# Low parts of w_in, key sums and both halves of a head's first keys made on VectorE instead of POOL

## The chip, the cores and the metric

The kernel runs on one core of a Trainium2 chip. Its metric is the device time of one execution in microseconds (us). Before the change it is 2476.84 us, the median of three runs (2475.95 to 2477.19). One further execution was taken by the hardware profiler; the profile's numbers come from that one.

The engines, by the names of the profile: PE is TensorE (matrix products; PEld are its weight loads), DVE is VectorE, ACT is ScalarE, POOL is GpSimd, SP is SyncE, which issues nearly all DMAs here. In the code they are `T`, `V`, `S`, `G` and `nc.sync`. Each engine runs its own queue of instructions strictly in order.

## The reference, cut to what matters

One layer of a diffusion backbone on 2048 latent tokens of width 1024, with 256 context tokens ahead:

```
h = modulate(rmsnorm(x), shift, scale)
p = h @ w_in                          # 1024 x 3584: gates fwd, gates bwd, v, q, out gate (512 each), u, v of the gMLP
k_f, k_b = sigmoid(-gate_f), sigmoid(-gate_b);  f = sigmoid(gate)
o = scan_fwd(q, k_f, v, f_f) + scan_bwd(q, k_b, v, f_b)      # gated linear recurrence, 4 heads of 128 x 128 state
o_hg = rmsnorm(o) * silu(p_gate);  o_mlp = spatial gating of u, v
x = x + g1 * (concat(o_hg, o_mlp) @ w_out)
x = x + g2 * conv_ffn(modulate(rmsnorm(x)))                  # up-projection, 3x3 depthwise conv, down-projection
return rmsnorm(x) * norm_final
```

All in fp32.

## The kernel before

**Split products.** TensorE's fast fp32 format (F32R) keeps fewer bits. So each factor is split in a high part, a rounded copy made by ScalarE, and a low part, what the copy lost: `lo = raw - hi` (`split`, line 129). A product is then three products: hi·hi, hi·lo, lo·hi (`mm3`, and the same three lines in `run_banks`, line 534).

**Stages.** By the trace's times: modulation vectors and context tokens (0 to some 180 us); projections and heads (to 1010 us); output projection and second norm (to some 1260 us); up-projection with the convolution (to 2048 us); down-projection and final norm (to the end). The change lies in the first two.

**Projections.** w_in is taken 128 columns at a time, a *key* in the code. `split_w` loads such a column (raw, 128 partitions x 8 x 128), lets ScalarE make `whi` and another engine `wlo`. There are two buffers for the pair: `w_free` holds the free ones. `run_banks` goes through a list of *banks*, products of one column with 512 (context: 256) tokens, 24 products each, with the result in a PSUM bank `pj`. At each bank it makes sure that this column and the one after it are split, so the split of a column waits until the products of the column two before it are done. A head's two gate columns are interleaved (`[ff[0], fb[0], ff[1], fb[1]]`, line 1018), so both buffers are held until the third of these four banks is done, and the column after them has one bank's time.

**Who makes the low part.** `split_w` counts its calls in `w_n` and takes VectorE for the first seven and every odd one below 20, POOL for the others (line 223). Two early calls name VectorE themselves.

**A head.** `hg` (line 775) is a generator whose steps are put between the banks' products by a pump, after waits in TensorE time that are written in the code (`yield 6.5`). First `kd`, the sum of both directions' keys, and `Q`, queries times gates of each direction; then score products with `kd` for the diagonal; then seven levels `B = 1, 2, 4 ... 64`. Each level has score products of `K` and `Q` (copied into `sc` through a mask by `V.copy_predicated`), an update of `Q` in place, new keys `K2` from `level_keys`, and the next totals. `level_keys` (line 562) makes the keys for B up to 32 in two halves, a = 0 and 1. Of each half one part is multiplied by totals, a = 0 on VectorE and a = 1 on POOL, and the other part is copied by ScalarE. At B = 1 the totals are the gates `F` themselves, and the copies are pinned in ScalarE's program order.

**Beside it** a second pump runs background work between the products: x's second half, modulation rows (`ada_block`, line 918), w_out and w_down times their gates (`w_out_ops`, line 950, which loads a gate row `g` from DRAM; `w_down_ops`, line 966).

**What sets the order.** When the program is built, a planner goes through it with times of its own and puts each instruction in its engine's queue when its inputs are ready by those times, earlier code first among ready ones. `pin` ties an instruction behind all earlier code of its engine. On the chip the queues are fixed: an instruction that must wait holds all behind it on its engine.

Of the kernel before, what the change touches and what calls it, by code (L numbers as in the profile page):

```python
# [24 lines left out]
CTX = 256  # L25
HW = 512
# [57 lines left out]
def tile_trunk(ctx, tc, x, c, cx, c_ctx, w_ada, b_ada, norm_mix, norm_ffn, w_in, hg_norm, sgu_g, sgu_b,  # L84
               w_sp, b_sp, w_out, w_up, conv_w, conv_b, w_down, norm_final, masks, out):
    nc = tc.nc
    V, S, G, T = nc.vector, nc.scalar, nc.gpsimd, Tensor(nc.tensor)
# [41 lines left out]
    def split(hi, lo, raw, eng=None, keep=lambda i: i):  # L129

        keep(S.copy(hi, raw))  # L131
        (eng or G).tensor_sub(lo, raw, hi.bitcast(F32))  # L132
# [56 lines left out]
    with es1:  # L189
# [13 lines left out]
        def bank(tag):  # L203
            return ps.tile([P, 512], F32, tag=tag, name=tag, bufs={"pj": 3, "sc": 2, "mi": 3}[tag])
# [1 line left out]
        def raw_tile():  # L206
            return p1.tile([P, D], F32, tag="raw", name="raw", bufs=3)

        w_n, w_raw, w_free = [0], {}, [0, 1]

        def load_raw(key):
            raw = raw_tile().rearrange("p (k c) -> p k c", c=P)
            ld(raw, w_in[:, key[0]:key[0] + P].rearrange("(k p) c -> p k c", p=P))
            w_raw[key] = raw

        def split_w(key, eng=None):
            if key not in w_raw:
                load_raw(key)
            raw, at = w_raw.pop(key), w_free.pop(0)
            hi = p1.tile([P, NK, P], F32R, tag=f"whi{at}", name="whi", align_bytes=AL)  # L220
            lo = p1.tile([P, NK, P], F32R, tag=f"wlo{at}", name="wlo", align_bytes=AL)
            w_n[0] += 1
            split(hi, lo, raw, eng or (V if w_n[0] < 8 or w_n[0] < 20 and w_n[0] % 2 else G))
            return hi, lo, at

        def x_sums():
            return pm.tile([P, 8], F32, tag="xss", name="xss", bufs=2)

        def x_square(xs, ss, i0=0, keep=pin):
            for i, xt in enumerate(xs):  # L230
                jk = pm.tile([P, D], BF16, tag="acc", name="xjk")
                keep(S.activation(jk, xt, AF.Square, accum_out=ss[:, i0 + i:i0 + i + 1]))

        def x_scale(xs, ss, keep=pin):

            r = rstd(pm, ss[:, :len(xs)], len(xs), 1.0 / D, keep=keep)
            for i, xt in enumerate(xs):
                keep(V.tensor_scalar(out=xt, in0=xt, scalar1=r[:, i:i + 1], scalar2=None, op0=ALU.mult))
# [18 lines left out]
        wts, rows, pa, nxt = {}, {}, {}, {}  # L257
# [5 lines left out]
        def load_ada(g, qs=(0, 1)):  # L263

            for q in (qs,) if isinstance(qs, int) else qs:
                t = wa[g // 2][:, 4 * (g % 2) + 2 * q:4 * (g % 2) + 2 * q + 2, :]
                wts[g, q] = t.rearrange("p a (b e) -> p (a b) e", e=512)
                ld(wts[g, q], wv[:, 4 * q:4 * q + 4, g * 512:(g + 1) * 512])
# [3 lines left out]
        def ada_products(g, k0, k1):  # L272
            if k0 == 0:
                pa[g] = bank("pj")
            for k in range(k0, k1):
                T.matmul(pa[g][:2, :], cs2[:, k, :], wts[g, k // 4][:, k % 4, :], start=(k == 0), stop=(k == 7))

        def ada_rows(g, tag):
            rows[g] = pm.tile([2, 512], F32, tag=tag, name="rows", bufs=2)
            S.copy(rows[g], pa.pop(g)[:2, :])  # L280

        def ada_columns(g):
            o = 128 + 16 * g
            for j in range(4):
                T.transpose(small[:, o + 2 * j:o + 2 * j + 2], rows[g][:, j * P:(j + 1) * P], ident[:2, :2])
            put_ada(g, small[:, o:o + 8].rearrange("p (j w) -> p w j", w=2), 0, 2)
# [36 lines left out]
        def ctx_products(c, ks):  # L323
            hi, lo, _ = nxt[c, CTX]
            pj = opened[c, CTX]
            for k in ks:
                mm3(pj[:, :CTX], hi[:, k, :], lo[:, k, :], chl[:, k, :], cll[:, k, :], k == 0, False)
# [4 lines left out]
        with tc.manual_schedule():  # L332
            load_ada(2)
            for i in range(2):
                ld(xc[i], cx[0][i * P:(i + 1) * P, :])
            vr = pm.tile([66, P], F32, tag="gu", name="vr", bufs=2)
            for a, n, r0 in ((norm_mix[0], 8, 0), (b_ada[0, 0:2 * D], 16, 50), (norm_ffn[0], 8, 8), (hg_norm[0], 4, 16),
                             (sgu_g[0], 4, 20), (sgu_b[0], 4, 24), (conv_b[0], 22, 28)):
                S.dma_start(vr[r0:r0 + n, :], a.rearrange("(r p) -> r p", p=P))
            load_ada(0)  # L340
            load_raw((0, CTX))
            load_ada(1)
            load_ada(3)
            load_raw((HW, CTX))
            S.activation(sg, cc, AF.Sigmoid)
            V.tensor_mul(cs2.rearrange("p k w -> p w k"), cc, sg)
            ss = x_sums()
            x_square(xc, ss, keep=lambda i: i)
            ada_products(2, 0, 4)
            small = bank("sc")  # L350
            T.transpose(small[:, :66], vr, ident[:66, :66])
            V.tensor_copy(vec, small[:, :50])
            V.tensor_copy(bc[:, :8], small[:, 50:58])
            V.tensor_scalar(out=bc[:, 8:], in0=small[:, 58:66], scalar1=1.0, scalar2=None, op0=ALU.add)
            ada_products(2, 4, 8)
            ada_rows(2, "ot")
            x_scale(xc, ss, keep=lambda i: i)
            ada_products(0, 0, 4)
            ada_columns(2)
            nxt[0, CTX] = split_w((0, CTX), V)  # L360
            for k in range(NK):
                for i in range(2):
                    o = (k % 2) * 256 + i * P
                    T.transpose(pct[k // 2][:, o:o + P], xc[i][:, k * P:(k + 1) * P], ident)
            ada_products(0, 4, 8)
            ada_rows(0, "ot")
            ada_sums(1, 0, 5)
            load_raw((2 * HW, CTX))
            for i in range(4):
                ld(xg[i], x_rows[i])  # L370
            ada_products(3, 0, 1)
            ada_columns(0)
            ada_products(3, 1, 8)
            ctx_mod(0)
            ada_sums(1, 5, 8)
            for k in range(1, 4):
                ctx_mod(k)
                ada_sums(0, k - 1, k)
            nxt[HW, CTX] = split_w((HW, CTX), V)
            ss0 = x_sums()  # L380
            x_square(xg[:1], ss0, keep=lambda i: i)
            ada_rows(3, "ot")
            ada_ones(1, small, 256)
            ada_columns(3)
            opened[0, CTX] = bank("pj")
            ctx_products(0, range(4))
            for k in range(4, NK):
                ctx_mod(k)
            ada_sums(0, 3, 8)
            ada_ones(0, small, 288)  # L390
# [171 lines left out]
        def level_keys(K, B, tot):  # L562

            W, nb = TH, TH // B
            K2 = pk.tile([P, 2, W], F32, tag="K", name="K2", bufs=2, align_bytes=AL)
            if B == P // 2:
                n = W // (2 * B)
                src = [[2 * B, n], [B, 2], [1, B]]
                t = view(tot, nb + 1, [[2, n], [-(nb + 1), 2], [0, B]])
                V.tensor_mul(view(K2, 0, [[2 * B, n], [W + B, 2], [1, B]]), view(K, 0, src), t)  # L570
                S.copy(view(K2, W, [[2 * B, n], [B - W, 2], [1, B]]), view(K, W, src))
                return K2
            n = W // (4 * B)
            for a in range(2):
                src = [[4 * B, n], [B, 2], [1, B]]
                t = view(tot, nb + 1 + 2 * a, [[4, n], [-(nb + 1), 2], [0, B]])
                e = G if a else V
                keep = pin if B == 1 else lambda i: i
                e.tensor_mul(view(K2, a * (2 * B + W), [[4 * B, n], [W + B - 2 * a * W, 2], [1, B]]),
                             view(K, a * 2 * B, src), t)  # L580
                keep(S.copy(view(K2, a * 2 * B + (1 - a) * W, [[4 * B, n], [B - W + 2 * a * W, 2], [1, B]]),
                            view(K, W + a * 2 * B, src)))
            return K2
# [60 lines left out]
        for h in range(NH):  # L644
            F, K, vt = sets[h % 2]
# [128 lines left out]

        def hg(hh, h, F, K, qs, vt, sgt):
            kd = ph.tile([P, TH], F32, tag="T1", name="kd")
            G.tensor_add(kd, K[:, 0, :], K[:, 1, :])
            Q = ph.tile([P, 2, TH], F32, tag="Q", name="Q", align_bytes=AL)
            for d in range(2):
                V.tensor_mul(Q[:, d, :], qs, F[:, d, :])  # L780
# [11 lines left out]
            for l, B in enumerate(LV):  # L792
# [13 lines left out]
                K = level_keys(K, B, tot)  # L806
# [522 lines left out]
    B = [[xah[:, i] if i < NR else None, xal[:, i] if i < NR - 1 else None] for i in range(7)]  # L1329
# [186 lines left out]
    for n, (u, i) in enumerate(prods):  # L1516
# [7 lines left out]
        hi, lo = u.A[i]  # L1524
# [37 lines left out]
    V = Kept(nc.vector, pin)  # L1562
# [243 lines left out]
```

## Time and profile before

| | us |
|---|---|
| median of three runs | 2476.84 |
| profiled execution | 2477.96 |
| its span, first to last instruction | 2476.2 |
| PE busy | 2421.4 (98%) |
| DVE busy | 1784.7 (72%) |
| ACT busy | 968.2 (39%) |
| POOL busy | 1053.7 (43%) |
| POOL's low parts of w_in, 55 | 135.5 |
| POOL's key sums, 8 | 26.0 |
| POOL's halves of the first keys, 8 | 21.1 |

A row of a group gives line, engine, operation, out<-in by the program's names, shape, count, then busy us, mean ns of one, and after the second bar the idle time of the engine just before these instructions with what ended it. A row of the timeline gives start, duration and, in brackets, the idle time before it and its releaser. Line 132 is the subtraction in `split`, line 131 its copy, line 65 any product. Products are pipelined and their ends modelled, so a product's duration is longer than the distance to the next.

### The profile page before, as it was taken

The page shows a single profiled execution, that of the slowest core. Times are in us where ns is not written, and L with a number is a line of the kernel's source. Part 1 is how long each engine was busy: PE and PEld are TensorE (multiplying, and loading weights), DVE is VectorE, ACT ScalarE, POOL GpSimd, SP SyncE. Part 2 cuts the span into 40 slices and gives each one's busy share as a digit, 9 for nine tenths or more (in the row PEclk, how much of TensorE's full clock was granted, in tenths as well). Part 3 has the DMA queues.
Part 4 walks back from the last instruction along what each step waited for, and adds up shares of the span by engine and source line. Part 5 has one row for each costly group of instructions (what it writes and reads, how often), then busy time and mean ns, then how long its engine had stood idle before and what let it go on. Part 6 is the DMA issues. An engine that isn't in the chain of part 4 may idle for free.

```text
span 2476.2 us, 32805 instructions
## 1 busy us (share of the span) xinstructions
PE 2421.4 (98%) x11859; PEld 2009.7 (81%) x11859; DVE 1784.7 (72%) x2374; ACT 968.2 (39%) x1614; POOL 1053.7 (43%) x866
## 2 busy tenths in 40 slices
PE   7899999999999999999999999999999999999998
PEld 4787888788888888788878888888878888888887
DVE  5766875645765866465699778759999993776876
ACT  3454334434344443244443333334333342432343
POOL 1344232332333433100588787887878770000002
PEclk9999999999999999999999999999999999999999
DMA  8365445573353422768932222472222239834645
GB/s 304 96 191 184 128 137 189 177 261 120 103 182 129 144 99 86 241 210 258 310 106 90 89 80 90 143 273 86 83 93 85 91 101 354 309 120 153 225 149 195
DMA packets 307854, 400.12 MB, mean 162 GB/s; under 512 B 33113, under 2 KB 216161, under 8 KB 304621
## 3 DMA queue, kind: packets, MB, share of 16 engines
q1 hardware_dynamic: 304404, 397.28, 48.3%
q8 instruction: 94, 1.54, 0.3%
q10 hardware_dynamic: 3289, 0.76, 0.1%
q14 instruction: 67, 0.55, 0.1%
HBM read 288.85 MB, written 109.13 MB: 161 GB/s over the span
## 4 chain that ended last, share of the span: by engine, by line
PE 37%; DVE 7%; issue 3%; POOL 2%; ACT 1%; DMA 1%; SPq 0%; POOLq 0%; ACTq 0%; DVEq 0%
PE up L65 23%; PE dn L65 14%; DVE dn L1373 3%; DVE edges L1378 1%; DVE gp L1454 1%; ACT dn L1370 1%; POOL Al L132 0%; DMA yd<-fl 0%; POOL ra L1665 0%; POOL rr L1666 0%; DVE keep L1448 0%; POOL raw L1191 0%; DVE keep L1464 0%; ACT Ah L131 0%; ACT cv L1392 0%
## 5 line engine op out<-in xcount | busy, mean ns | idle before, releaser
L1373 DVE SCALAR_TENSOR_TENSOR dn<-gp,taps,dn 128x1024 f32<-128x1024 f32 x352 | 448.6, 1281 | 21.1 <-ACT dn L1370 17.9
L65 PE MATMUL up<-yf,Ah 128*128 128x512 f32 x1232 | 393.5, 389 | 0.0
L65 PE MATMUL dn<-thl,mhl 128*128 128x512 f32 x1680 | 381.5, 389 | 1.2 <-ACT thl L131 1.2
L132 POOL TENSOR_TENSOR Al<-raw,Ah 128x512 fp32r<-128x512 f32 x264 | 343.0, 1308 | 89.5 <-ACT Ah L131 81.4
L65 PEld LDWEIGHTS dn<-thl,mhl 128*128 128x128 f32 x1680 | 315.0, 188 | 67.7 <-ACT thl L131 2.0
L65 PE MATMUL pj<-xh,whi 128*128 128x512 f32 x896 | 363.8, 406 | 0.0
L65 PE MATMUL pj<-xh,wlo 128*128 128x512 f32 x896 | 350.8, 392 | 1.2 <-DVE wlo L132 1.2
L65 PE MATMUL pj<-xl,whi 128*128 128x512 f32 x896 | 350.3, 391 | 1.2 <-POOL xl L132 1.0
L65 PE MATMUL up<-xah,Al 128*128 128x512 f32 x704 | 275.5, 391 | 3.4 <-POOL Al L132 3.1
L65 PE MATMUL up<-xah,Ah 128*128 128x512 f32 x704 | 274.6, 390 | 0.6 <-ACT Ah L131 0.6
L65 PEld LDWEIGHTS up<-yf,Ah 128*128 128x128 f32 x1232 | 231.2, 188 | 47.9
L131 ACT CAST Ah<-raw 128x512 fp32r<-128x512 f32 x264 | 160.6, 618 | 276.3 <-PE up L65 213.7
L132 POOL TENSOR_TENSOR wlo<-raw,whi 128x1024 fp32r<-128x1024 f32 x55 | 135.5, 2464 | 250.3 <-ACT whi L131 224.3
L65 PE MATMUL up<-xal,Ah 128*128 128x512 f32 x528 | 205.5, 389 | 0.0
L65 PE MATMUL up<-yf,Al 128*128 128x512 f32 x528 | 205.2, 389 | 0.0
L65 PEld LDWEIGHTS pj<-xh,wlo 128*128 128x128 f32 x896 | 168.3, 188 | 37.5 <-DVE wlo L132 1.7
L65 PEld LDWEIGHTS pj<-xh,whi 128*128 128x128 f32 x896 | 168.8, 188 | 32.8 <-issue 3.5
L65 PEld LDWEIGHTS pj<-xl,whi 128*128 128x128 f32 x896 | 168.9, 189 | 31.8 <-POOL xl L132 1.8
L65 PE MATMUL dn<-wo,o 128*128 128x512 f32 x768 | 182.9, 394 | 1.8 <-DVE nt L706 0.9
L65 PEld LDWEIGHTS dn<-wo,o 128*128 128x128 f32 x768 | 141.9, 188 | 31.7 <-issue 1.1
L65 PEld LDWEIGHTS up<-xah,Al 128*128 128x128 f32 x704 | 132.1, 188 | 36.0 <-POOL Al L132 8.6
L1665 POOL TENSOR_SCALAR ra<-ss 128x1 f32<-128x1 f32 x8 | 5.3, 662 | 359.8 <-ACT jk L1657 359.8
(317 smaller groups left out, 4186.9 us busy)
## 6 DMA issues: line engine op xcount, KB each, us to landing
raw<-in_w_up_dram SPq DMA_DIRECT2D x88, 512.0 KB, 4.5
mr<-m SPq DMA_DIRECT2D x85, 512.0 KB, 5.3
raw<-in_w_in_dram SPq DMA_DIRECT2D x68, 512.0 KB, 4.3
sT<-wd SPq DMA_DIRECT2D x88, 256.0 KB, 4.4
raw<-in_w_ada_dram SPq DMA_DIRECT2D x32, 512.0 KB, 3.9
yf<-yd SPq DMA_DIRECT2D x14, 1024.0 KB
m<-cv SPq DMA_DIRECT2D x22, 544.0 KB, 2.7
raw<-in_w_down_dram SPq DMA_DIRECT2D x22, 512.0 KB, 3.8
```

Source lines behind the costliest of these rows:

```text
L65: return self.engine.matmul(out, lhsT, rhs, **kw)
L131: keep(S.copy(hi, raw))
L132: (eng or G).tensor_sub(lo, raw, hi.bitcast(F32))
L1370: S.activation(cr, gt[:, 0:RH, 0:GW], AF.Identity, bias=cvb[:, f:f + 1], scale=taps[:, f:f + 1])
L1373: V.scalar_tensor_tensor(out=cr, in0=gt[:, t // 3:t // 3 + RH, t % 3:t % 3 + GW], scalar=taps[:, t * NF + f:t * NF + f + 1], in1=cr, op0=A ...
L1378: V.scalar_tensor_tensor(out=e[:, 0, :], in0=gt[:, 1, t % 3:t % 3 + GW], scalar=taps[:, t * NF + f:t * NF + f + 1], in1=e[:, 0, :], op0=AL ...
L1454: V.tensor_add(g_rows(hh, f + c, n2), quad(p, kind), quad(add, kind))
L1665: G.tensor_scalar(out=a, in0=ss, scalar1=plus, scalar2=None, op0=ALU.add)
```

## The change

Three kinds of instructions go from POOL to VectorE:

- `split_w` always names VectorE; the counter `w_n` and the parameter `eng` go. 55 low parts move, 13 were there before.
- `kd`, the sum of both directions' keys, once in each of the 8 heads (4 heads, two halves of the tokens).
- at B = 1 of `level_keys` the half a = 1, so that VectorE makes both halves; from B = 2 on POOL keeps its half.

No arithmetic, buffer, DMA or product is added or removed, and nothing is moved in the code; since the planner sees other engines, the order in the queues can differ.

```diff
-        w_n, w_raw, w_free = [0], {}, [0, 1]
+        w_raw, w_free = {}, [0, 1]
...
-        def split_w(key, eng=None):
+        def split_w(key):
...
-            w_n[0] += 1
-            split(hi, lo, raw, eng or (V if w_n[0] < 8 or w_n[0] < 20 and w_n[0] % 2 else G))
+            split(hi, lo, raw, V)
             return hi, lo, at
...
-            nxt[0, CTX] = split_w((0, CTX), V)
+            nxt[0, CTX] = split_w((0, CTX))
...
-            nxt[HW, CTX] = split_w((HW, CTX), V)
+            nxt[HW, CTX] = split_w((HW, CTX))
...
                 t = view(tot, nb + 1 + 2 * a, [[4, n], [-(nb + 1), 2], [0, B]])
-                e = G if a else V
+                e = G if a and B > 1 else V
                 keep = pin if B == 1 else lambda i: i
...
             kd = ph.tile([P, TH], F32, tag="T1", name="kd")
-            G.tensor_add(kd, K[:, 0, :], K[:, 1, :])
+            V.tensor_add(kd, K[:, 0, :], K[:, 1, :])
```

## The prediction

> **What bounds the kernel now.** I read the page's busy shares first, then the chain of waits, a table by stage, what TensorE itself waited for, and last the moved instructions one by one. The page's first part gives busy time, share of the span and count:
>
> ```profile
> PE 2421.4 (98%) x11859; PEld 2009.7 (81%) x11859; DVE 1784.7 (72%) x2374; ACT 968.2 (39%) x1614; POOL 1053.7 (43%) x866
> ```
>
> TensorE is the bound, and the change gives it no work and takes none. Only a wait of TensorE can be won or made. The chain of waits, in order of time, starts behind the projections and heads, so it tells nothing of the stage where all moved instructions lie; its longest early piece does show what follows that stage:
>
> ```profile
> 1259.33 367.06 PE up L65 x1618
> ```
>
> 1618 products run there without a break. What TensorE ends earlier before that, I take to arrive whole at the end.
>
> Two stretches of a table by stage (stretch, length, busy time of PE, PEld, DVE, ACT, POOL):
>
> ```profile
> 60.00:180.00 120.00, 111.44 (x660) 95.50 (x659) 86.30 (x167) 62.77 (x113) 45.66 (x38) 0.99 0.44 139
> 180.00:1010.00 830.00, 810.30 (x4567) 696.29 (x4566) 548.38 (x821) 330.50 (x596) 291.47 (x195) 1.00 0.46 152
> ```
>
> TensorE idles 8.6 us in the first and 19.7 us in the second: 28.3 us, 1.1% of the span, is all that other engines can give back here. VectorE idles 830 - 548 = 282 us in the second, so it has room in the mean; the question is the order within it. TensorE's own waits from 60 to 1010 us (total, times, longest):
>
> ```profile
> PE mi L69 <- ACT vv L588: 3.3, 3, 1.9
> PE sc L65 <- ACT K L581: 3.0, 2, 1.8
> PE mi L69 <- DVE xfl L243: 2.9, 3, 1.1
> PE mi L69 <- DVE xk L238: 2.6, 3, 1.9
> PE sc L65 <- DVE Q L501: 2.5, 5, 1.3
> PE pj L65 <- DVE wlo L132: 1.7, 3, 0.9
> ...
> PE sc L65 <- POOL kd L777: 1.3, 2, 0.7
> ```
>
> No row names a low part made on POOL: TensorE never waited visibly for those that move. It waited 1.3 us for key sums, and 3.0 us for ScalarE's copies of keys, which stand behind POOL's halves.
>
> **The change, part by part.** The moved instructions and their neighbours (by tile: min/median/max ns and count; by group: busy us, mean ns):
>
> ```profile
> L132 POOL TENSOR_TENSOR wlo<-raw,whi x55: 2349/2401/3468, 69.7 to 966.8; 128x1024 fp32r<-128x1024 f32 x55
> L132 DVE TENSOR_TENSOR wlo<-raw,whi x13: 1210/1220/2048, 21.4 to 177.7; 128x1024 fp32r<-128x1024 f32 x13
> L777 POOL TENSOR_TENSOR kd<-K x8: 2374/3374/3393, 228.5 to 899.2; 128x1024 f32<-128x1024 f32 x8
> L579 POOL TENSOR_TENSOR K<-K,F 128x512 f32<-128x512 f32 x8 | 21.1, 2638 | 0.0
> L579 DVE TENSOR_TENSOR K<-K,F 128x512 f32<-128x512 f32 x8 | 20.7, 2592 | 0.0
> L780 DVE TENSOR_TENSOR Q<-qs,F 128x1024 f32<-128x1024 f32 x16 | 34.3, 2160 | 43.3 <-ACT F L554 43.2
> ```
>
> The start of the first head, from the timeline (start, us, engine, line):
>
> ```profile
> 225.94 2.58 POOL L132 TENSOR_TENSOR wlo<-raw,whi 128x1024 fp32r<-128x1024 f32 x1 [2.62 <-ACT whi L131]
> 226.38 3.22 DVE L780 TENSOR_TENSOR Q<-qs,F 128x1024 f32<-128x1024 f32 x1
> 228.48 3.38 POOL L777 TENSOR_TENSOR kd<-K 128x1024 f32<-128x1024 f32 x1
> 232.33 1.11 DVE L579 TENSOR_TENSOR K<-K,F 128x512 f32<-128x512 f32 x1
> ...
> 240.04 2.40 POOL L132 TENSOR_TENSOR wlo<-raw,whi 128x1024 fp32r<-128x1024 f32 x1 [8.18 <-ACT whi L131]
> 240.35 1.19 ACT L581 COPY K<-K 128x512 f32<-128x512 f32 x1
> 242.34 2.22 DVE L501 TENSOR_TENSOR Q<-Q,F 128x1024 f32<-128x1024 f32 x1
> 242.39 3.81 POOL L579 TENSOR_TENSOR K<-K,F 128x512 f32<-128x512 f32 x1
> 246.24 1.15 ACT L581 COPY K<-K 128x512 f32<-128x512 f32 x1 [4.69 <-POOL K L579]
> ```
>
> *Load.* VectorE gets 55 low parts at 1.22 us (67 us); 8 key sums of 1024 columns, which it nowhere makes now and which I price like the low part of that size (10 us; at most 2.16 us each, the mean of the equally large Q product); and 8 second halves at 1.11 us, as the first half of 232.33 (9 us; at most 2.59 each). Together 86 us. It gets time back: the Q product of 226.38 ended at 229.60, 1.1 us behind the end of POOL's low part (228.52), as if it had started only then. If all 16 Q products fall from 2.16 to 1.22 us, 15 us come back. Net some 70 of 282 idle us, none of it on TensorE's path by size alone. POOL loses 55 x 2.4 + 26 + 21, about 180 us, and no one waits longer for what it keeps.
>
> The Trainium skill, page "SBUF — State Buffer", section "Who interferes with whom", states that a VectorE instruction with two SBUF inputs and a GpSimd instruction that reads SBUF shut each other out for a whole instruction. The Q product agrees (3.22 us). By that rule the low part remains exposed on VectorE to POOL's halves of the later levels, as its 2048 ns maximum suggests: at worst 55 x 0.83 = 46 us more load, by an estimate, where the sum here has none.
>
> *Key sums.* POOL's kd stood behind a low part and ended at 231.86. On VectorE: low part 225.9 to 227.2, Q to 228.4, kd to 229.6. That is 2.3 us earlier, more than the longest wait (0.7 us). Won: 1.3 us; bounds 0 and 1.3.
>
> *First keys.* The halves don't run side by side. First half, ScalarE's copy, second half, second copy follow each other, since all four write one tile; the waits show it at the later levels:
>
> ```profile
> POOL K L579 <- ACT K L581: 59.0, 21, 6.8
> ```
>
> So the second half cannot start on VectorE before 241.54 (240.35 + 1.19), and the wait for ScalarE's copy now stands in VectorE's queue, with the mask copies and the update of Q behind it. Their readers are TensorE's next score products. Placed ahead of that update, and behind a low part of 1.22 us, the half ends near 244, 2 us before POOL's 246.20, and the 1.8 us wait goes. Placed behind the update (2.22 us), it ends near 246.4 and nothing is won. I take 2.0 of the 3.0 us, nearer the first; bounds 3.0, and -1.1 where the half delays Q.
>
> *Behind ScalarE.* The value copies queue behind the key copies, and TensorE waits for them:
>
> ```profile
> 449.46 0.65 ACT L581 COPY K<-K 128x512 f32<-128x512 f32 x1 [1.63 <-POOL K L579]
> ...
> 451.14 0.55 PE L69 MATMUL mi<-ident,vv 128*128 128x128 f32 x3 [1.86 <-ACT vv L588]
> ```
>
> That copy belongs to a later level, whose half stays on POOL, but it starts earlier if the first level ends earlier. I take 1.6 of 3.3 us; bounds 0 and 3.3.
>
> *Before 180 us.* One moved low part lies where VectorE is crowded (86 of 120 us):
>
> ```profile
> 69.68 3.38 POOL L132 TENSOR_TENSOR wlo<-raw,whi 128x1024 fp32r<-128x1024 f32 x1
> 71.45 2.16 DVE L132 TENSOR_TENSOR xl<-xfl,xh 128x512 fp32r<-128x512 f32 x1
> ```
>
> It adds 1.22 us to VectorE, and the low part of x beside it, which ended just behind it (73.61 against 73.06), falls by about 1.5 us to some 0.7, since it then waits for nothing. The row scaling xk that TensorE waited 1.9 us for stands behind both, and its factor comes from POOL, where 3.38 us go. Won 1.0 of 2.6 us; bounds -1.2 and 2.6. Of the 2.5 us for Q updates I take 0.8, as fewer are pushed back by POOL; bounds 0 and 2.5.
>
> Sum of gains: 1.3 + 2.0 + 1.6 + 1.0 + 0.8 = 6.7 us.
>
> *The price of the queue.* A low part waits for its high part on ScalarE, which waits for TensorE to free the buffer; POOL stood idle meanwhile (8.18 us at 240.04), VectorE would not. The planner puts it where its own times say that the high part is ready, so VectorE loses only what these times miss. It also stands behind whatever waits there, above all the w_out products that wait for a gate row:
>
> ```profile
> DVE raw L950 <- DMA raw<-g_d: 29.3, 12, 9.8
> ...
> 417.25 2.41 POOL L132 TENSOR_TENSOR wlo<-raw,whi 128x1024 fp32r<-128x1024 f32 x1 [19.61 <-ACT whi L131]
> 422.64 0.69 DVE L950 TENSOR_TENSOR raw<-raw 128x512 f32<-128x512 f32 x1 [9.76 <-DMA raw<-g_d]
> ```
>
> VectorE stands still from 412.9 to 422.64 for that row. The low part ready at 417.25 serves the column right behind the gates' last bank: 24 products of 367.06 / 1618 = 0.227 us, 5.4 us after its high part could start (416.1), so it is wanted from about 422. Behind the waiting row it ends at 424.5, behind a Q product too at 425.8. TensorE would lose 2.5 to 3.8 us, less what other products are put between; ahead of the row, nothing. I take 2.0; bounds 0 and 3.8. For the other 54, VectorE's own rows give the bounds: 13 low parts there made TensorE wait 1.7 us, 0.13 us each, which is 7.1 us for 54; POOL's 55, asked for at the same distance and 1.2 us longer each, made it wait for none. I take 1.0, nearer the second row, as VectorE has idle time there.
>
> **The sum.** 6.7 - 2.0 - 1.0 = 3.7 us. The profiled execution took 2477.96 us (span 2476.2 and 1.8 around it), 1.1 us above the median of the three runs, 2476.84. 2477.96 - 3.7 = 2474.3 us on the profile's scale, 2473.1 on that of the median: forecast 2473, 0.15% faster.
>
> **The rivals.** A difference under 0.2%, 5 us, can hardly be told from none.
>
> *A: the whole relief reaches TensorE.* VectorE runs the chain of a head's start without POOL's blocks, ScalarE is held less, and the waits on ACT vv, ACT K, DVE xk, DVE Q and POOL kd go: 3.3 + 3.0 + 2.6 + 2.5 + 1.3 = 12.7 us. With 2 us given back in the queue it ends 10.7 us lower, 2466. For it: two of the largest waits hang on the first keys. Against it: half of that sum belongs to later levels, where POOL keeps its halves, and to the gate rows that hold VectorE anyway.
>
> *B: VectorE's queue becomes the bound at the weights; slower.* The low part is asked for one bank after its buffer comes free; POOL, in idle waiting, always made it. VectorE comes to it behind mask copies, level updates and waits for DMA. Price: 0.13 us for each of 55, 7.2 us, plus 3.8 us at 417, 11.0 us, against key sums and ScalarE's copies alone as gain (1.3 + 2.0): 7.7 us slower, 2484.5. It decides from a mean delay of TensorE of 6.7 / 55 = 0.12 us per low part, where it eats the gains. Against it: 282 us of idle VectorE, and 1.2 us more room per low part than POOL had.
>
> *C: nothing reaches TensorE.* The second half still stands behind ScalarE's copy, so the series keeps its length and the change doesn't do what its move promises; the key sums' 1.3 us are eaten in the queue. 2476.8.
>
> **How the numbers follow.** Chances: forecast 0.40, A 0.25, B 0.18, C 0.17. The forecast's own spread, 2470 to 2476, leaves a third of it below 2471.9. Faster: 0.25 + 0.13 = 0.38; within 0.2%: 0.27 + 0.17 = 0.44; slower: 0.18. The range goes from 3 us under A, if the waits for xfl go too (2.9 us), to 2484, where half of B ends: 2463 to 2484. The bounds of the single terms, taken all at their bad ends, reach past it (-1.1 - 1.2 - 3.8 - 7.1 is 13 us), but they don't share a cause.
>
> **What would show each step.** Right: no low part and no key sum on POOL, POOL's busy time down by about 180 us; Q products near 1.2 us; TensorE's waits on the key sum and on ScalarE's copy of keys gone; the second half of the first keys some 2 us nearer the first copy; a wait of VectorE for whi, in total under 50 us. Wrong: more than 5 us of TensorE waiting for wlo on VectorE (B), a second half that still ends 4 us behind the first copy (C), idle time of TensorE from 60 to 1010 us under 20 us (A). The forecast falls altogether if the new order moves waits behind 1010 us, where I count none.

## The result, and the profile after

The changed kernel takes 2460.49 us (median of 4 runs, 2459.64 to 2464.26) against 2477.02 for the kernel before on the same chip (4 runs, 2475.95 to 2480.83): ratio 0.9931, 95% interval 0.9916 to 0.9946. It is 16.5 us faster, 12.5 us below the forecast of 2473 and below the range of 2463 to 2484. The profiled execution took 2459.64 us with a span of 2457.9, 18.3 less than before. Below line 222 the line numbers are one lower than before (L579 is L578, and so on).

Busy times of the whole execution, from the page:

```profile
PE 2417.9 (98%) x11859; PEld 2008.3 (82%) x11859; DVE 1790.2 (73%) x2445; ACT 970.5 (39%) x1614; POOL 882.5 (36%) x795
```

POOL loses 171 us. VectorE took on 55 low parts, 8 key sums and 8 halves, and its busy time rose by 5.5 us only. The moved rows give what it took on (instructions by tile):

```profile
L132 DVE TENSOR_TENSOR wlo<-raw,whi x68: 1209/1224/2042, 21.6 to 949.9; 128x1024 fp32r<-128x1024 f32 x68
L776 DVE TENSOR_TENSOR kd<-K x8: 1211/1217/1226, 218.4 to 881.6; 128x1024 f32<-128x1024 f32 x8
```

55 x 1.22 + 8 x 1.22 + 8 x 1.14 (the mean of both halves, below) is 86 us. So 80 us came back to VectorE from work that was not moved. A group of the kernel before that the prediction did not quote (busy us, mean ns), and the same and two others after:

```profile
L918 DVE SCALAR_TENSOR_TENSOR acc<-raw,cs,acc 128x512 f32<-128x512 f32 x64 | 63.7, 995 | 3.4 <-DMA acc<-in_b_ada_dram 2.7
```

```profile
L917 DVE SCALAR_TENSOR_TENSOR acc<-raw,cs,acc 128x512 f32<-128x512 f32 x64 | 50.6, 790 | 1.3 <-DMA raw<-in_w_ada_dram 0.8
L779 DVE TENSOR_TENSOR Q<-qs,F 128x1024 f32<-128x1024 f32 x16 | 19.2, 1216 | 0.0
L578 DVE TENSOR_TENSOR K<-K,F 128x512 f32<-128x512 f32 x16 | 18.3, 1144 | 0.0
```

The Q products fell from 34.3 to 19.2 us, the accumulations of w_ada from 63.7 to 50.6, VectorE's half of the first keys from 2.59 to 1.14 us each (the mean of both halves now): together some 40 of the 80 us. All three are products or sums that take two operands from SBUF; the rest is spread over smaller groups.

The stages (stretch, length, busy time of PE, PEld, DVE, ACT, POOL), as before:

```profile
60.00:180.00 120.00, 116.48 (x688) 99.43 (x688) 91.36 (x190) 64.77 (x119) 33.09 (x35) 1.00 0.50 155
180.00:1010.00 830.00, 818.39 (x4601) 703.52 (x4600) 553.28 (x869) 332.89 (x594) 131.97 (x126) 1.00 0.48 157
```

TensorE idles 3.5 us in the first stretch (8.6 before) and 11.6 in the second (19.7): 13.1 of the 18.3 us. Its busy time for the same 11859 products is another 3.5 lower; that part is not shown to be the change's, since the mean granted clock of TensorE was 0.996 in the profile before and 0.998 in this one. Where the gain has arrived is read from a product that occurs in every head, the first and the last start of it; before it stood at 232.3 and 910.7:

```profile
L65 PE MATMUL sc<-qs,kd x128: 272/275/275, 223.1 to 892.5; 128*128 128x128 f32 x128
```

9.2 us are won by the first head, ahead of which ten low parts and the head's own key sum have moved, and 18.2 by the last.

TensorE's waits from 60 to 1010 us (total, times, longest):

```profile
PE pj L65 <- DVE wlo L132: 3.6, 3, 2.1
PE sc L65 <- ACT K L580: 3.1, 6, 0.8
...
PE sc L65 <- DVE Q L500: 1.1, 1, 1.1
...
PE mi L69 <- DVE xfl L242: 0.7, 2, 0.4
PE mi L69 <- DVE xk L237: 0.3, 1, 0.3
```

The waits for the value copies (3.3 us) and the key sums (1.3) are gone, xk fell from 2.6 to 0.3, xfl from 2.9 to 0.7, Q from 2.5 to 1.1. Low parts rose from 1.7 to 3.6, and the wait for ScalarE's copies of keys did not go: 3.0 in two waits before, 3.1 in six now.

The crowded place of the prediction, about 70 us, from the timeline after:

```profile
67.19 1.29 POOL L132 TENSOR_TENSOR xl<-xfl,xh 128x512 fp32r<-128x512 f32 x1 [4.40 <-ACT xh L131]
67.52 2.04 DVE L132 TENSOR_TENSOR wlo<-raw,whi 128x1024 fp32r<-128x1024 f32 x1
...
70.20 0.67 DVE L132 TENSOR_TENSOR xl<-xfl,xh 128x512 fp32r<-128x512 f32 x1
70.80 1.21 DVE L132 TENSOR_TENSOR wlo<-raw,whi 128x1024 fp32r<-128x1024 f32 x1
```

The low part of x falls from 2.16 to 0.67 us, as forecast, now that no low part on POOL (3.38 us) runs beside it. The first low part still shows what such an overlap does: beside POOL's xl, which ends at 68.48, it takes 2.04 us instead of 1.21.

### The profile page after: what moved, and what is told of

Same layout as the page of the kernel before. It is cut to its first block, busy times and chain, and to the rows that moved or that the text cites. A ratio compares the mean times of both kernels' runs of the same rounds, so it can differ in the third digit from the quotient of the medians.

```text
span 2457.9 us, 32777 instructions
## 1 busy us (share of the span) xinstructions
PE 2417.9 (98%) x11859; PEld 2008.3 (82%) x11859; DVE 1790.2 (73%) x2445; ACT 970.5 (39%) x1614; POOL 882.5 (36%) x795
## 4 chain that ended last, share of the span: by engine, by line
PE 45%; DVE 7%; issue 3%; POOL 2%; ACT 2%; DMA 1%; SPq 0%; POOLq 0%; ACTq 0%; DVEq 0%
PE up L65 24%; PE dn L65 20%; DVE dn L1372 3%; DVE edges L1377 1%; DVE gp L1453 1%; ACT dn L1369 1%; POOL Al L132 1%; PE up L69 0%; PE pj L65 0%; POOL ra L1664 0%; DMA raw<-oT 0%; DMA xn<-cv 0%; POOL rr L1665 0%; DMA raw<-in_w_up_dram 0%; DVE keep L1447 0%
## 5 line engine op out<-in xcount | busy, mean ns | idle before, releaser
L578 POOL TENSOR_TENSOR K<-K,tot 128x512 f32<-128x512 f32 x40 | 57.4, 1434 | 306.4 <-ACT K L580 222.4
L132 DVE TENSOR_TENSOR wlo<-raw,whi 128x1024 fp32r<-128x1024 f32 x68 | 83.8, 1232 | 99.7 <-ACT whi L131 93.4
```

## The experiments

Two theories were tried first. Theory L: a POOL instruction that reads SBUF holds up VectorE's instructions with two SBUF operands, and taking POOL's low parts away frees VectorE. Theory S: the series at a head's start (key sum, first keys) carries the gain. A third, O, puts it down to the new order of instructions.

### One part at a time

Low parts alone (before, with one line changed):

```diff
-            split(hi, lo, raw, eng or (V if w_n[0] < 8 or w_n[0] < 20 and w_n[0] % 2 else G))
+            split(hi, lo, raw, V)
```

> The kernel before with all 68 low parts of w_in's columns on VectorE; key sums and second halves of the first keys stay on POOL. Theory L (a POOL instruction that reads SBUF holds up VectorE's products of two SBUF operands, so 55 low parts of 2.4 us gone from POOL free VectorE): 11 to 14 us faster than before, 2463 to 2466; the Q products of qs and F fall from 2.16 us to under 1.6 us, and TensorE's idle time from 60 to 180 us from 8.6 to under 5. Theory S (the series of a head's start, which runs over key sums and first keys, carries the gain): 0 to 4 us faster, 2473 to 2477. The prediction's terms for this part alone (+1.6 +1.0 +0.8 -3.0): no change, 2476.6. Theory O (the planner's new order carries the gain, whatever is moved): any time, and the three parts do not add to 16.5 us.

Measured: 2457.37 us (4 runs, 2455.52 to 2459.26) against 2477.17; ratio 0.9921, 0.9904 to 0.9937. This part alone brings 19.8 us, more than the whole change.

Key sums alone, and the second halves of the first keys alone:

```diff
-            G.tensor_add(kd, K[:, 0, :], K[:, 1, :])
+            V.tensor_add(kd, K[:, 0, :], K[:, 1, :])
```

```diff
-                e = G if a else V
+                e = G if a and B > 1 else V
```

> The kernel before with the sums of both directions' keys on VectorE, nothing else moved. Theory L: POOL loses 8 x 3.4 us, VectorE gains 8 x 1.2; 0 to 2 us faster, 2475 to 2477. Theory S: 5 us and more faster, under 2472, since a head's first score product gets its operand sooner. The prediction's term: 1.3 us faster, 2475.7.

> The kernel before with the second halves of the first keys on VectorE, nothing else moved. Theory L: 0 to 3 us faster, 2474 to 2477. Theory S: 5 us and more faster, under 2472. The prediction's term: 2.0 us faster, and part of the 1.6 us behind ScalarE's copies: 2474.

Measured: 2473.01 us for the sums (10 runs, 2469.99 to 2476.39; ratio 0.9985, 0.9975 to 0.9994), 2474.79 for the halves (10 runs, 2472.82 to 2478.12; 0.9991, 0.9982 to 1.0). The sums bring 4.2 us, more than L or the prediction gave them; the halves' 2.4 us cannot be told from nothing. With theirs beside 19.8, S as the carrier is out. The order of TensorE's instructions with the sums moved is the one of before, so that gain owes nothing to it. Nor does it come from the wait that was named for it: TensorE waited 2.0 us for key sums there, against 1.3 before. What fits L is that VectorE took on 8 sums (10.4 us) and was yet 2.0 us less busy (1782.7). The three parts add to 26.4, not 16.5: something is lost when they stand together (further down).

Only the early low parts, six in number:

```diff
-            split(hi, lo, raw, eng or (V if w_n[0] < 8 or w_n[0] < 20 and w_n[0] % 2 else G))
+            split(hi, lo, raw, eng or (V if w_n[0] < 20 else G))
```

> The kernel before with only the 6 or 7 low parts on VectorE that lie before about 180 us; the later ones, the key sums and the keys stay on POOL. Theory L with the trace after (the start of the first head is 8.1 us nearer there, before any key sum or key that was moved): 6 to 9 us faster, 2468 to 2471. Theory S: nothing, 2477. The prediction's term for this stretch: 1.0 us, 2476.

Measured: 2470.26 us (9 runs, 2468.29 to 2475.51; 0.9979, 0.9969 to 0.9989), 6.9 us faster, from six instructions of POOL. The product sc<-qs,kd starts 8.3 us earlier in the first head and 7.8 in the last, so it is won there and kept (up to 3 us of the 8.3 may be scatter: with the sums or the halves alone, and no low part moved, it started 1.4 and 3.1 us earlier):

```profile
L65 PE MATMUL sc<-qs,kd x128: 272/275/377, 224.0 to 902.9; 128*128 128x128 f32 x128
```

### POOL reads, or POOL is merely busy

Both kernels start from the low parts alone and put work that nobody reads at the 55 places where POOL made low parts. The first reads the high part:

```diff
-        w_n, w_raw, w_free = [0], {}, [0, 1]
+        w_n, w_raw, w_free = [0], {}, [0, 1]; scr = pm.tile([P, 4, P], BF16, name='scr')
...
-            split(hi, lo, raw, V)
+            split(hi, lo, raw, V), (w_n[0] < 8 or w_n[0] < 20 and w_n[0] % 2) or ([G.tensor_sub(scr, hi[:, j:j + 4].bitcast(F32), hi[:, j:j + 4].bitcast(F32)) for j in (0, 4)])
```

The second, with the same scratch tile, reads one column and then only writes:

```diff
-            split(hi, lo, raw, V)
+            split(hi, lo, raw, V), (w_n[0] < 8 or w_n[0] < 20 and w_n[0] % 2) or (G.tensor_copy(scr[:, 0, :1], hi[:, 0, :1].bitcast(F32)), [G.memset(scr, 0.0) for j in range(5)])
```

The instructions of TensorE, VectorE, ScalarE and SyncE stand in the same order in these two and in the kernel they start from; only POOL's queue differs.

> The kernel with only the low parts moved (measured at 2457.4 us against 2477.2 before), and at each of the 55 places where POOL made a low part before, POOL now takes the difference of the high part with itself, in two halves of 512 columns, into a scratch tile that nobody reads. The order of all instructions of the other engines stays as without them, and the extra work is read by no one. Theory L (POOL's reading holds up VectorE): most of the 19.8 us is lost again, 2470 to 2485, and the Q products of qs and F rise from 1.49 us to 1.8 or more. Theory P (what was won is POOL's own queue: its keys, sums and low parts of x no longer stand behind low parts): also 2470 and more, but the Q products stay at 1.5 us. Theory T (the low part is simply ready 1.2 us sooner on VectorE): 2457 to 2460.

> As the run with the reading decoy, but at each of the 55 places POOL reads one column of the high part and then fills the scratch tile five times, so that it is occupied about as long and hardly reads. Theory L: nothing is lost, 2456 to 2461, Q products near 1.5 us. Theory P: as much is lost as with the reading decoy, 2470 and more. Theory T: 2457 to 2460. So L and P are told apart by this run, L and T by the other.

Measured: reading 2482.02 us (10 runs, 2479.94 to 2486.11; ratio 1.0018, 1.0009 to 1.0027), writing 2459.76 (4 runs, 2457.85 to 2460.16; 0.9921, 0.9904 to 0.9937). Reading loses all that the low parts had won and ends 4.5 us behind the kernel before (2477.53 beside these runs), with more reading on POOL than there (164.5 against 135.5 us); writing stays within 2.4 us of the low parts alone. Busy times and the added instructions, reading:

```profile
PE 2421.7 (98%) x11859; PEld 2011.7 (81%) x11859; DVE 1831.8 (74%) x2429; ACT 968.0 (39%) x1614; POOL 1097.6 (44%) x921
...
L223 POOL TENSOR_TENSOR scr<-whi 128x512 bf16<-128x512 f32 x110 | 164.5, 1495 | 239.1 <-ACT whi L131 235.7
L780 DVE TENSOR_TENSOR Q<-qs,F 128x1024 f32<-128x1024 f32 x16 | 29.8, 1878 | 0.0
```

and writing:

```profile
PE 2417.2 (98%) x11859; PEld 2011.0 (82%) x11859; DVE 1790.9 (73%) x2429; ACT 969.4 (39%) x1614; POOL 1102.8 (45%) x1141
...
L223 POOL MEMSET scr<- 128x512 bf16 x275 | 145.4, 529 | 13.9
...
L780 DVE TENSOR_TENSOR Q<-qs,F 128x1024 f32<-128x1024 f32 x16 | 21.4, 1354 | 0.0
```

POOL is as busy in the one as in the other (1097.6 and 1102.8 us), and VectorE, with the same 2429 instructions, works 41 us longer where POOL reads. TensorE idles 28.9 us from 60 to 1010 us where POOL reads and 14.1 where it writes (11.5 with the low parts alone). One and the same low part in the two timelines, reading and then writing:

```profile
276.57 2.71 POOL L223 TENSOR_TENSOR scr<-whi 128x512 bf16<-128x512 f32 x2 [7.97 <-ACT whi L131]
276.85 1.53 DVE L918 SCALAR_TENSOR_TENSOR acc<-raw,cs,acc 128x512 f32<-128x512 f32 x1
278.30 2.06 DVE L132 TENSOR_TENSOR wlo<-raw,whi 128x1024 fp32r<-128x1024 f32 x1
```

```profile
270.30 0.75 DVE L918 SCALAR_TENSOR_TENSOR acc<-raw,cs,acc 128x512 f32<-128x512 f32 x1
270.49 2.86 POOL L223 MEMSET scr<- 128x512 bf16 x5
270.96 1.22 DVE L132 TENSOR_TENSOR wlo<-raw,whi 128x1024 fp32r<-128x1024 f32 x1
```

1.53 and 2.06 us beside reading, 0.75 and 1.22 beside writing. That excludes POOL's queue (P), the earlier end of the low part (T) and the order (O) as the carrier, and shows that POOL's reading is. Another way for it to cost, that the extra reader holds the buffer of the high part, is out too: ScalarE waited 5.8 us for the extra work before its next high part where it reads, 8.7 where it writes.

L is not the whole of it, though. Where POOL reads, its own instructions grow longer as well: its second halves of the first keys take 3.33 us in the mean, 1.97 where it writes. ScalarE's copies stand behind them, and TensorE's waits for them are its largest in the reading run (total, times, longest), where the writing run has no such row:

```profile
PE sc L65 <- ACT K L581: 7.8, 5, 2.6
```

How much of the loss comes by VectorE's instructions and how much by POOL's was not separated.

The Trainium skill, page "SBUF — State Buffer", section "Who interferes with whom", states that a VectorE instruction with two SBUF inputs contends with a GpSimd instruction that reads SBUF, and not with one that only writes it. These two runs agree with both halves of it.

### Where 3 us are lost when all is moved

In the trace after, the second half of the first keys stands behind the update of Q in VectorE's queue (timeline):

```profile
532.32 1.20 ACT L580 COPY K<-K 128x512 f32<-128x512 f32 x1
...
534.93 2.23 DVE L500 TENSOR_TENSOR Q<-Q,F 128x1024 f32<-128x1024 f32 x1
536.98 1.16 DVE L578 TENSOR_TENSOR K<-K,F 128x512 f32<-128x512 f32 x1
538.17 1.22 ACT L580 COPY K<-K 128x512 f32<-128x512 f32 x1 [4.66 <-DVE K L578]
...
539.45 2.19 PE L65 MATMUL sc<-Q,K 128*128 128x128 f32 x16 [0.81 <-ACT K L580]
```

The same head with the low parts alone, where POOL keeps that half:

```profile
528.17 1.20 ACT L581 COPY K<-K 128x512 f32<-128x512 f32 x1
529.45 1.95 POOL L579 TENSOR_TENSOR K<-K,F 128x512 f32<-128x512 f32 x1 [10.42 <-ACT K L581]
530.81 2.69 DVE L501 TENSOR_TENSOR Q<-Q,F 128x1024 f32<-128x1024 f32 x1
531.43 1.21 ACT L581 COPY K<-K 128x512 f32<-128x512 f32 x1 [2.06 <-POOL K L579]
```

POOL, free of low parts, starts as the first copy ends and is done at 531.40, 2.0 us behind it; VectorE is done at 538.14, 4.6 us behind it. This head is not alone: in the trace after, the half stands behind the update of Q in five of the eight heads and ends 4.6 to 4.8 us behind the first copy there, 1.3 to 3.3 in the other three; with the low parts alone it is 1.9 to 2.7 in all eight. Two kernels add one part each to the low parts, and both ends were run again on the same chip:

> Low parts and key sums on VectorE, the second halves of the first keys on POOL. Theory L alone: POOL loses 22.8 us more of reading, so 0 to 3 us faster than with the low parts alone, 2455 to 2457. If VectorE's queue sets the price of every further instruction: 2459 to 2461.

> Low parts and the second halves of the first keys on VectorE, key sums on POOL. Theory F (in the trace after, the second half stands behind the update of Q in VectorE's queue and ends 4.6 us behind the first copy, where POOL, free of low parts, ends it 2.1 us behind; TensorE then waits 3.1 us for ScalarE's copies of keys, where it waits none with the low parts alone): 2 to 4 us slower than with the low parts alone, 2460 to 2462, with a row of waits for ScalarE's copies of keys. Theory L alone: 0 to 2 us faster, 2455 to 2457.

> The kernel with only the low parts moved, once more, on the same chip as the whole change: 2457, as before. If the whole change and the low parts alone are the same, both come to the same within 2 us; by theory F the low parts alone are 2 to 4 us faster.

> The changed kernel once more, all three parts on VectorE: 2460.5, as measured; by theory F 2 to 4 us above the low parts alone.

Measured, beside 2476.85 for the kernel before:

| on VectorE | us | runs | ratio, 95% interval |
|---|---|---|---|
| low parts | 2456.09 | 2454.88 to 2457.89 | 0.9915, 0.9901 to 0.9928 |
| low parts, sums | 2458.16 | 2455.68 to 2460.93 | 0.9925, 0.9911 to 0.9938 |
| low parts, first keys | 2460.95 | 2460.81 to 2461.71 | 0.9934, 0.9922 to 0.9947 |
| all three | 2459.44 | 2457.87 to 2461.33 | 0.9928, 0.9915 to 0.9940 |

The first keys cost 4.9 us on top of the low parts; the runs of the one and of the other do not overlap. Their wait is there whenever they are moved (this row is of low parts and first keys), and no such row stands among the waits with the low parts alone:

```profile
PE sc L65 <- ACT K L581: 3.3, 6, 0.8
```

That wait accounts for 3.3 of the 4.9 us. For the sums, 2.1 us, the runs overlap and nothing is settled. So of the 9.9 us between 26.4 and 16.5, the 6.6 of sums and halves are not won a second time once the low parts are gone, and some 3 are lost when both are added. The low parts alone are 3.1 and 3.4 us faster than all three in the two comparisons; the intervals of the ratios overlap, so that this kernel beats the changed one is likely, not certain.

### Two tries at more

The low parts of x on VectorE too, and, apart from it, the gate rows of w_out on POOL, both on top of the low parts alone:

```diff
-                x_mod(pt, 0, k, xh[:, k, sl], xl[:, k, sl], 512, V if k % 2 else G)
+                x_mod(pt, 0, k, xh[:, k, sl], xl[:, k, sl], 512, V)
...
-                        x_mod(pt[:, sl], 0, k + kk, sp[:, b, sl], sp[:, b + 1, sl], 256, V if kk else G)
+                        x_mod(pt[:, sl], 0, k + kk, sp[:, b, sl], sp[:, b + 1, sl], 256, V)
```

```diff
-                    V.tensor_mul(w, w, g)
+                    G.tensor_mul(w, w, g)
```

> The kernel with only the low parts of w_in's columns moved, and the low parts of the modulated x that POOL still makes (8 of 512 columns, 12.6 us, and 16 of 256, 18.2 us) on VectorE too. Theory L, in proportion to POOL's time (19.8 us for 135.5): 4 us faster than without, 2453. By the price of VectorE's queue (these parts lie where TensorE waits for xfl and xk): 2457 to 2460.

> The kernel with only the low parts of w_in's columns moved, and the 16 products of w_out's first rows with the gate row on POOL, so that VectorE no longer stands still for that row (23.9 us of waits in all). The prediction's price of the queue (2.0 us for the low part behind that wait): 2 to 3 us faster than without, 2455. Theory L: 16 products of 512 columns on POOL hold VectorE up in turn, 21 us of POOL's time at 19.8 for 135.5 is 3 us; so no gain, 2457 to 2460.

Measured: 2457.88 us (0.9915, 0.9901 to 0.9930) and 2467.66 (0.9956, 0.9941 to 0.9971). The first brings nothing beside 2457.4. So the proportion in L's expectation was wrong; the run doesn't tell whether POOL's reading costs nothing at these places, or VectorE's queue takes back what is won (its busy time rises from 1788.8 to 1795.7 us). The second loses 10 us, which neither number foresaw. TensorE has three waits there that the low parts alone don't have: 3.1 us for a key sum and twice 3.4 us for ScalarE's copies (vv and gv), 9.9 us in all. The first can be followed in the timeline:

```profile
408.48 1.29 POOL L950 TENSOR_TENSOR raw<-raw 128x512 f32<-128x512 f32 x1 [11.94 <-DMA raw<-g_d]
...
416.07 2.34 POOL L777 TENSOR_TENSOR kd<-K 128x1024 f32<-128x1024 f32 x1
...
418.46 2.05 PE L65 MATMUL sc<-qs,kd 128*128 128x128 f32 x16 [3.13 <-POOL kd L777]
```

The wait for the gate row only moved to POOL, and the key sum stands behind it there. What held the two copies was not followed.

## Why the prediction was wrong, step by step

*What bounds it.* Right: TensorE, and what is won before 1010 us arrives at the end (18.2 us at the last head, 18.3 at the end).

*Load: the step that failed.* "If all 16 Q products fall from 2.16 to 1.22 us, 15 us come back. Net some 70 of 282 idle us, none of it on TensorE's path by size alone." The Q products did exactly that, but 80 us came back and the net is 5.5. The contention had been read from one row (226.38) and paid out to one group, when other VectorE groups with two SBUF operands stood under POOL's reading too: the accumulations of w_ada (13.1 us came back) and VectorE's half of the first keys (11.6). And beyond 1.0 us before 180 us and 0.8 for Q updates, what came back was put at nothing on TensorE's path, while the low parts alone, which the terms of the sum left at about no change, gave 19.8 us. The rule of the Trainium skill cited there was turned against the change only (46 us more load), not added up for it: VectorE was priced as if the 55 instructions were a load, when their place on POOL was the larger one. Not all of it was the low parts' doing: with these alone the Q products still took 1.49 us, and 1.22 only with the key sums moved as well.

*Before 180 us.* "One moved low part lies where VectorE is crowded". Two groups of the stretch from 60 to 180 us show what was missed, before and after:

```profile
L132 DVE TENSOR_TENSOR wlo<-raw,whi 128x1024 fp32r<-128x1024 f32 x8 | 10.6, 1322 | 4.5 <-ACT whi L131 4.5
```

```profile
L132 DVE TENSOR_TENSOR wlo<-raw,whi 128x1024 fp32r<-128x1024 f32 x15 | 19.1, 1272 | 7.5 <-ACT whi L131 5.5 <-DMA xl_d<-sp 1.9
```

Six of the moved low parts lie there, not one (the row after has seven more, because one from behind 180 us has come in with everything earlier). The term was 1.0 us with a bound of 2.6; these six alone measured 6.9. The other 49 come to 12.9 us by difference, where the terms for them (1.6 + 0.8 - 3.0) made a loss of 0.6. Waits for xfl, put at nothing, gave 2.2 of their 2.9 us.

*First keys.* 2.0 us of gain, bounds 3.0 and -1.1. The case "Placed behind the update (2.22 us), it ends near 246.4 and nothing is won" came about in five of the eight heads. Since POOL's half had become prompt by itself, the move costs: 4.9 us on top of the low parts. A move that cures a delay was priced as if the other part of the change had not cured it already. The delay had also been read from one head: POOL's half ended 4.7 us behind the first copy there, but 2.7 in four of the eight heads before.

*Key sums.* 1.3 us; 4.2 measured alone, by another way than the wait that was to go, and not told from nothing on top of the low parts. In the trace after TensorE's wait for them is gone, as forecast.

*Behind ScalarE.* 1.6 of 3.3 us were taken; all 3.3 went, but not for the reason given, a first level that ends earlier: they went with the low parts alone too, where no first key moved, and in the head of the row shown there the second half still ends 4.8 us behind the first copy (4.7 before). That is luck. *Q updates*: 0.8 taken, 1.4 went.

*The price of the queue.* Mechanism and place were right: the low part behind the gate row held TensorE for 2.1 us, forecast 2.0. The close size is luck: the repeat of this kernel had 1.1 us as its longest wait for a low part. The rows of the trace after:

```profile
410.46 0.69 DVE L949 TENSOR_TENSOR raw<-raw 128x512 f32<-128x512 f32 x1 [10.54 <-DMA raw<-g_d]
411.07 1.22 DVE L132 TENSOR_TENSOR wlo<-raw,whi 128x1024 fp32r<-128x1024 f32 x1
...
412.34 0.50 PE L65 MATMUL pj<-xh,wlo 128*128 128x512 f32 x1 [2.11 <-DVE wlo L132]
```

All waits for low parts rose by 1.9 us, where 3.0 were forecast; B, the queue as the bound, did not come. VectorE's waits for high parts came to 93 us, not "in total under 50 us", and TensorE waited for low parts no longer than said.

*The rivals.* A came nearest and had half the mechanism, "VectorE runs the chain of a head's start without POOL's blocks"; the sign that was named for it came, idle time of TensorE of 15.1 us. But it hung two of its largest waits on the first keys, whose move lost time; the wait for ScalarE's copies of keys stayed (3.1 us), and it gave nothing to the stretch ahead of the heads beyond xk. C's sign came as well, "a second half that still ends 4 us behind the first copy", in five of eight heads; C was right about that part alone.

## What to carry to other kernels

In this kernel, work on POOL that reads SBUF is not free while VectorE has products or sums of two SBUF operands to do: POOL was only 43% busy and TensorE never waited for its low parts, yet their 135.5 us cost 19.8 us. Before pricing a move between the two, compare the mean of each such VectorE group with its shortest instance, add up the difference, and look at where VectorE is the most crowded. Over all of VectorE's groups up to 1260 us the sum is 127 us in the trace before and 59 in the trace after. It bounds what VectorE can get back, and is not the gain of the kernel: 80 us came back here, and 16.5 reached the end. And price the parts of a change one after another, since the second may move work out of a place that the first has already cleared.

## What was not expected of the hardware

That filling a tile on POOL, 275 times 529 ns, is all but free for VectorE (busy time 1790.9 us against 1788.8 without) was theory L's expectation. What was not expected is how much POOL's own instructions change: its key sums of 1024 columns took 3.24 us in the mean before and 2.85 with the low parts gone, its halves of the first keys 2.64 and 1.99. That they are held up by VectorE in turn fits, but no run isolates it. And the row scaling xk, which takes one tile and a factor per row, was also shorter, 925 ns in the mean before and 746 after:

```profile
L238 DVE TENSOR_SCALAR xk<-xk,rs 128x1024 f32<-128x1024 f32 x12 | 10.5, 925 | 3.4 <-POOL rs L126 3.4
```

With the reading work added it was 877, with the writing work 776; what holds up an instruction of one tile was not looked into.
